# Moving the scaled copies of x and their trips behind the block's work on yi in a Mamba-2 scan, with the masked cb ahead of them

## The chip, the cores and the metric

The kernel runs on one core of one Trainium2 chip. The metric is the device time of one execution in microseconds (us). The engines are TensorE (PE, with its weight loads shown apart as PEld), VectorE (DVE), ScalarE (ACT), GpSimd (POOL) and SyncE (SP, which here only issues DMAs). Each engine works through its own list of instructions in order; when an instruction waits for a semaphore, everything behind it on that engine waits too.

## The reference

One layer of a hybrid network is computed for 256 frames of a new stream and 8 x 16 frames of running streams, 384 rows of 2048 in all, in float32:

```
u = RMSNorm(x);  P = u @ w_in            (columns: pool | z | x, B, C | dt | gates)
branch A: windowed means minus self, a linear map per group, a scale
branch B: x, B, C = silu(causal_conv(...));  y = ssd_scan(x, dt, A, B, C, h0) + D * x
          a = RMSNorm_per_group(y * silu(z))
m = sigmoid(gA) * (A @ w_pool_proj) + sigmoid(gB) * (a @ w_ssd_proj)
x += RMSNorm(m @ w_out);  x += RMSNorm(relu(RMSNorm(x) @ w_up)^2 @ w_down)
```

The change lies in the scan. Per group of heads it is, for a chunk with decays `cum`:

```
cb    = C @ B^T                                  (within the chunk)
y     = (cb * decay) @ (x * dt)  +  (C @ h) * exp(cum)
h_new = h * exp(last) + B^T @ (x * dt * w_end)
```

## The kernel before

The product with every weight is made of three matmuls: weight and activation are each split into a high and a low part, and high-high, high-low and low-high are added up (`mm3`). Weights come in half tiles of 128 x 1024 over SP's DMA queue (`wfetch`, line 63). ScalarE makes the high part (`wh`, line 70), VectorE the low part (`wl`, line 71); each of the three buffers in the chain has three slots. A projection of one 128-column tile uses two such halves of 24 matmuls (`half`, lines 98 to 100).

The phases are: the input norm and the pool branch (to about 410 us), the scan (to about 1220 us), the B gates, the output projections, and the MLP. The scan runs over 8 blocks, one for each of the 8 groups of heads; a block has 10 projections: two tiles of x, then B, C, two more tiles of x, and four of z. Its heads are handled as two pairs of x tiles, `D.p[0]` (called S) and `D.p[1]` (called S1). The code for S1 runs on into the next block as `prev.p[1]`.

Steps of the scan that matter here, by the names in the code:

- `conv` (a projection, `conv_in`, and `taps`): the result goes into `cbuf` (line 581), three taps are added in `cacc` (line 597) and a SiLU gives the tile `xs`.
- `xturned`: x is transposed within 32 x 32 blocks on VectorE (`xb`, line 612), spread to memory by four DMAs on POOL's queue (line 617) and fetched back as `xT` (line 623). The steps are placed one by one behind the halves of the next projections (`tick`).
- `xside`: from `xT` VectorE makes `xdt` and scales `xT` itself (line 738, four products of 128 x 384 for a pair), and `yis` from `yi` (line 745). The scaled `xT` is split into `xhl` (high part on ScalarE, line 752, low part on VectorE, line 753). Two DMAs on SP's queue take rows of it to memory (`x_scr`, line 756) and eight bring them back in another layout (`xst`, line 760).
- `mside`: VectorE multiplies `cb`, which lies in a PSUM bank, with the mask (`cbm`, line 731).
- `eside`: ScalarE builds the decays `E`, VectorE multiplies them with `cbm` (line 782). `dside` scales the state `hs` (line 785).
- On TensorE: `t_pp` (line 696, reads `xhl`), `t_cb` (line 652), `t_yT` (line 674, reads `yis`), `t_Y` (line 682, reads `xdt` and `E`), `t_yi` (line 661) and, in `state`, `t_su` (line 800, reads `xst` and `bst`), whose sums VectorE adds to `hs` (line 809). `final` gives `xs` (line 824) and the gated products (line 832).
- `bside` splits the transposed B (`Bhl`, lines 708 and 709) and sends it on its own trip through memory (lines 711 and 715).

In a block these TensorE steps stand in two bunches (`lump` keeps their order): after the projection of the third x tile come `t_pp` of the block before, `t_cb`, `t_yT` and `t_Y` of the block before, `t_yi` of S and `t_su` of the block before; after the last z projection come the same steps for S and `t_yi` for S1.

PSUM has two banks of tag `mm` (projections and `py`) and six of tag `ss` (`cb`, `Y`, `su` and others). `xT`, `xhl`, `xst`, `yis` and `cbm` have one buffer each, `xdt` two.

What sets the order: TensorE's order in the scan is that of the code (`last`, `chain`, `behind`). For the other engines a planner in the tile framework orders the instructions before the run. It goes by its own estimate of when an instruction is ready; of several that are ready, the one that stands earlier in the program goes first. A tile is handed on when its last reader is done.

Of the kernel before, what the change touches and what calls it, by code (L numbers as in the profile page):

```python
# [6 lines left out]
F32 = mybir.dt.float32  # L7
# [3 lines left out]
ALU = mybir.AluOpType  # L11
# [3 lines left out]
P = 128  # L15
# [18 lines left out]
def build(ctx, tc, io):  # L34
    nc = tc.nc
    v, s, te, gp, sy = nc.vector, nc.scalar, nc.tensor, nc.gpsimd, nc.sync
# [323 lines left out]
    tok = small.tile([P, 11, NH], F32, name="tok")  # L360
    decb = small.tile([P, NH, NB], F32, name="decb")
    with tc.tile_pool(name="phc", bufs=1, reuse_waits="tile") as pc, tc.tile_pool(name="phc2", bufs=2, reuse_waits="tile") as pc2:
        pst = pc.tile([P, KD, NB, 15], F32, name="pst")
        gp.dma_start(pst, io["state_pool"])
        bufs = []
# [192 lines left out]
    with tc.tile_pool(name="phd", bufs=2, reuse_waits="tile") as pd, tc.tile_pool(  # L558
        name="phd1", bufs=1, reuse_waits="tile"
# [32 lines left out]
        def taps(b, c, tag, nb):  # L592
            a = pd.tile([P, T], F32, tag="cacc", name=f"cacc{c}")
            w = lambda j: vec[:, V_CW + c * 4 + j : V_CW + c * 4 + j + 1]
            s.activation(seg(a), b[:, :, 0:16], AF.Copy, scale=w(0))
            for j in range(1, 4):
                v.scalar_tensor_tensor(
                    out=seg(a), in0=b[:, :, j : j + 16], scalar=w(j), in1=seg(a), op0=ALU.mult, op1=ALU.add
                )
            o = pd.tile([P, T], F32, tag=tag, name=f"xs{c}", bufs=nb)  # L600
            s.activation(o, a, AF.Silu, bias=vec[:, V_CB + c : V_CB + c + 1])
            return o

        def conv(ui, c, tag, nb):
            return taps(conv_in(ui, c), c, tag, nb)
# [19 lines left out]
        def xturned(D, g, j):  # L625
            S = D.p[j // 2]
            if j % 2 == 0:
                S.xT = pd.tile([P, 2, 3, P], F32, tag="xT", name=f"xT{S.nm}", bufs=1)
            turned(D.xs[j], g * 4 + j, S.xT[:, j % 2])
# [99 lines left out]
        def mside(D):  # L729
            D.cbm = pd.tile([P, 512], F32, tag="cbm", name=f"cbm{D.g}", bufs=1)  # L730
            v.tensor_tensor(D.cbm, D.cb, cst[:, C_MASK : C_MASK + 512], ALU.mult)

        def xside(S):
            S.xdt = pd.tile([P, 2, 3, P], F32, tag="xdt", name=f"xdt{S.nm}")
            for q in range(2):
                tv = S.xT[:, q].rearrange("p b (h q) -> p b h q", h=2)
                for o, i in ((S.xdt, 3), (S.xT, 6)):
                    v.tensor_tensor(
                        o[:, q].rearrange("p b (h q) -> p b h q", h=2),
                        tv,  # L740
                        tok[:, i : i + 3, S.h0 + q * 2 : S.h0 + q * 2 + 2].unsqueeze(3).to_broadcast([P, 3, 2, 64]),
                        ALU.mult,
                    )
            S.yis = pd.tile([P, 2, P], F32, tag="yis", name=f"yis{S.nm}", bufs=1)
            v.tensor_tensor(
                S.yis.rearrange("p j (h q) -> p (j h) q", h=2),
                S.yi.rearrange("p (h q) -> p h q", h=4),
                tok[:, 10, S.h0 : S.h0 + 4].unsqueeze(2).to_broadcast([P, 4, 64]),
                ALU.mult,
            )  # L750
            S.xhl = pd.tile([P, 2, 2, 3, P], F32R, tag="xhl", name=f"xhl{S.nm}", bufs=1)
            s.activation(S.xhl[:, 0], S.xT, AF.Copy)
            v.tensor_tensor(S.xhl[:, 1], S.xT, S.xhl[:, 0].bitcast(F32), ALU.subtract)
            xscr = x_scr[S.qd]
            for l in range(2):
                sy.dma_start(xscr[:, l], S.xhl[:, l, :, 2, :].bitcast(F32))
            S.xst = pd.tile([P, 4, 2 * P], F32R, tag="xst", name=f"xst{S.nm}", bufs=1)
            for p4 in range(4):
                for h2 in range(2):
                    sy.dma_start(  # L760
                        S.xst[h2 * 64 + p4 * 16 : h2 * 64 + p4 * 16 + 16].bitcast(F32),
                        xscr.rearrange("(q h r) l j n -> h l r q (j n)", q=4, h=2)[h2, p4 % 2],
                    )

        def eside(S, q):
            if q == 0:
                S.E = pd.tile([P, 4, 512], F32, tag="E", name=f"E{S.nm}", bufs=1)
            for hh in (q * 2, q * 2 + 1):
                ch = S.cbcs[q][:, hh % 2]
                s.activation(S.E[:, hh, P:TP], ch[:, P:TP], AF.Exp, bias=tok[:, 9, S.h0 + hh : S.h0 + hh + 1])  # L770
                for b, e0 in enumerate((0, TP, T)):
                    s.activation(
                        S.E[:, hh, e0 : e0 + P],
                        ch[:, b * P : b * P + P],
                        AF.Relu,
                        bias=tok[:, b, S.h0 + hh : S.h0 + hh + 1],
                        scale=-1.0,
                    )
            Eq = S.E[:, q * 2 : q * 2 + 2]
            s.activation(Eq[:, :, :P], Eq[:, :, :P], AF.Exp, scale=-1.0)  # L780
            s.activation(Eq[:, :, TP:], Eq[:, :, TP:], AF.Exp, scale=-1.0)
            v.tensor_tensor(Eq, Eq, S.D.cbm.unsqueeze(1).to_broadcast([P, 2, 512]), ALU.mult)
# [82 lines left out]
        prev = None  # L865
        for g in range(G + 1):
            if g == G:
                eside(prev.p[1], 0)
                eside(prev.p[1], 1)
                dside(prev.p[1])  # L870
                gate_b(0, pd, "hs")
                py = mmtile("pp_last")
                lump(lambda: t_pp(prev.p[1], py))
                lump(lambda: t_yT(prev.p[1]))
                lump(lambda: t_Y(prev.p[1]))
                state(prev.p[1])
                final(prev.p[1])
                gate_b(1, pd, "hs")
                finish(prev)
                break  # L880
            u0 = 17 + g * 10
            D = Pair()
            D.g = g
            D.p = [pair(D, jp) for jp in range(2)]
            D.xs, D.zs = [], []
            D.Bhl = pd.tile([P, 2, 3, P], F32R, tag="Bhl", name=f"Bhl{g}")
            D.xs.append(conv(u0, g * 4, "xs", 6))
            xturned(D, g, 0)
            pload(D.p[0])
            if g:  # L890
                eside(prev.p[1], 0)
            D.xs.append(conv(u0 + 1, g * 4 + 1, "xs", 6))
            xturned(D, g, 1)
            if g:
                eside(prev.p[1], 1)
            D.BT = conv(u0 + 2, 32 + g, "BT", 2)
            turned(D.BT, 32 + g, D.Bhl[:, 1].bitcast(F32))
            if g:
                dside(prev.p[1])
            cload(D.p[0])  # L900
            D.CT = conv(u0 + 3, 40 + g, "CT", 2)
            cside(D)
            b2 = conv_in(u0 + 4, g * 4 + 2)
            S = D.p[0]
            S.py = mmtile(f"py{S.nm}")
            if g:
                lump(lambda: t_pp(prev.p[1], S.py))
            lump(lambda: t_cb(D))
            bside(D)
            if g:  # L910
                lump(lambda: t_yT(prev.p[1]))
                lump(lambda: t_Y(prev.p[1]))
            lump(lambda: t_yi(S))
            xside(S)
            mside(D)
            if g:
                state(prev.p[1])
                final(prev.p[1])
            D.xs.append(taps(b2, g * 4 + 2, "xs", 6))
            xturned(D, g, 2)  # L920
            D.xs.append(conv(u0 + 5, g * 4 + 3, "xs", 6))
            xturned(D, g, 3)
            eside(S, 0)

            def zproj(j):
                ps = proj(in_units(u0 + 6 + j), xg, f"z{g}_{j}")
                z = pd.tile([P, T], F32, tag="zs", name=f"zs{g}_{j}", bufs=7)
                with later():
                    v.tensor_tensor(halves(z), even_odd(ps), halves(rstd), ALU.mult)  # L929
                    s.activation(z, z, AF.Silu)  # L930
                D.zs.append(z)

            zproj(0)
            pload(D.p[1])
            eside(S, 1)
            zproj(1)
            if g:
                finish(prev)
            zproj(2)
            dside(S)  # L940
            cload(D.p[1])
            zproj(3)
            S1 = D.p[1]
            S1.py = mmtile(f"py{S1.nm}")
            lump(lambda: t_pp(S, S1.py))
            lump(lambda: t_yT(S))
            lump(lambda: t_Y(S))
            lump(lambda: t_yi(S1))
            xside(S1)
            state(S)  # L950
            final(S)
            prev = D
# [92 lines left out]
    with tc.tile_pool(name="phf", bufs=1, side="right", reuse_waits="tile") as pf, tc.tile_pool(  # L1045
        name="phf2", bufs=2, side="right", reuse_waits="tile"
# [240 lines left out]
    with tc.tile_pool(name="phg", bufs=1, reuse_waits="tile") as pg, tc.tile_pool(  # L1287
# [9 lines left out]
        for c8 in range(NC):  # L1297
            hh = []
            for f8 in range(8):
                f = c8 * 8 + f8  # L1300
# [172 lines left out]
```

## Time and profile before

| | us |
|---|---|
| median of 3 runs | 2701.65 (2698.83 to 2708.1) |
| profiled execution, its own time | 2702.03 |
| span of the profile | 2700.1 |
| mean granted TensorE clock | 0.993 |

In the page, "busy" is the time in which an engine executed; a group's line is that of the kernel file. In a timeline row come the start in us from the begin of the span, the duration, the engine, the line, the operation, the tile written and those read, the shapes and a count; a bracket gives the idle time of the engine just before, and what ended it. In a row of the waits come the instruction that waited, what it waited for, the time in total, how often, and the longest. In a row of stretches come the busy times of the engines, each with its number of instructions, then the granted TensorE clock as a share of full speed, the busy share of the DMA engines and the GB/s. The whole page has TensorE at 98% and VectorE at 56% of the span; the scan, where the change lies, is one third of it.

### The profile page before, as it was taken

How to read it: one execution, taken by the hardware profiler on the slowest of the kernel's cores; microseconds unless marked ns; L12 is line 12 of the kernel's file. 1: busy time of each engine (PE TensorE's matmuls, PEld its weight loads, DVE VectorE, ACT ScalarE, POOL GpSimd, SP SyncE). 2: the span in 40 equal slices, each digit the busy share in tenths (PEclk: the TensorE clock that was granted, in tenths of full speed). 3: DMA queues.
4: the chain of work that ended last, by engine and by line, in shares of the span. 5: the costliest groups of instructions: out<-in, count | busy, mean ns of one | idle time of the engine just before them, and what ended most of it. 6: DMA issues, size and time to landing. Idle time of an engine off the chain costs nothing.

```text
span 2700.1 us, 38584 instructions
## 1 busy us (share of the span) xinstructions
PE 2647.5 (98%) x15149; PEld 2463.7 (91%) x15149; DVE 1524.7 (56%) x2148; ACT 1150.1 (43%) x1806; POOL 245.2 (9%) x366
## 2 busy tenths in 40 slices
PE   9999999899999899999999999999999999999998
PEld 9998889898999899988888888989999999999897
DVE  6585336687787787866433345634444444444446
ACT  6443235456565565644422234633233333333233
POOL 0000002223223223311000000000000000000000
PEclk9999999999999999999999999999999999999999
DMA  7444446666666676766644454333334444444443
GB/s 269 152 132 157 145 151 210 201 222 224 228 228 221 207 249 209 226 205 225 230 156 156 156 187 156 125 133 135 138 133 137 137 133 136 138 133 138 135 133 132
DMA packets 153845, 467.10 MB, mean 173 GB/s; under 512 B 21120, under 2 KB 48320, under 8 KB 148672
## 3 DMA queue, kind: packets, MB, share of 16 engines
q1 hardware_dynamic: 134400, 389.90, 44.1%
q0 software_dynamic: 19264, 74.74, 8.0%
q8 instruction: 119, 1.95, 0.3%
q14 instruction: 62, 0.51, 0.1%
HBM read 414.97 MB, written 49.58 MB: 172 GB/s over the span
## 4 chain that ended last, share of the span: by engine, by line
PE 55%; DVE 2%; DMA 1%; issue 1%; ACT 0%; POOL 0%; DVEq 0%; POOLq 0%; ACTq 0%
PE pj_up L98 6%; PE pj_up L100 6%; PE pj_up L99 6%; PE wd L151 6%; PE wd L150 6%; PE wd L149 6%; PE pj_sp L149 3%; PE pj_sp L150 3%; PE pj_sp L151 3%; PE wo L151 2%; PE wo L150 2%; PE pj_gb L149 2%; PE wo L149 2%; PE pj_gb L151 2%; PE pj_gb L150 2%
## 5 line engine op out<-in xcount | busy, mean ns | idle before, releaser
L98 PE MATMUL pj_up<-x1h,wh_up 128*128 128x384 f32 (+1 forms) x1024 | 333.7, 326 | 0.0
L99 PE MATMUL pj_up<-x1l,wh_up 128*128 128x384 f32 (+1 forms) x1024 | 333.4, 326 | 0.0
L100 PE MATMUL pj_up<-x1h,wl_up 128*128 128x384 f32 (+1 forms) x1024 | 333.4, 326 | 0.0
L71 DVE TENSOR_TENSOR wl_wd<-w_wd,wh_wd 128x1024 fp32r<-128x1024 f32 x126 | 154.3, 1225 | 240.5 <-ACT wh_wd L70 240.5
L149 PE MATMUL wd<-wh_wd,hh 128*128 128x512 f32 x756 | 286.5, 379 | 0.0
L150 PE MATMUL wd<-wl_wd,hh 128*128 128x512 f32 x756 | 286.5, 379 | 0.0
L151 PE MATMUL wd<-wh_wd,hl 128*128 128x512 f32 x756 | 286.5, 379 | 0.0
L70 ACT ACTIVATE wh_wd<-w_wd 128x1024 fp32r<-128x1024 f32 x126 | 133.1, 1057 | 322.3 <-PE wd L151 261.9
L98 PE MATMUL pj_x<-xgh,wh_x 128*128 128x384 f32 x768 | 256.1, 333 | 2.6 <-DVE zs L929 2.6
L70 ACT ACTIVATE wh_up<-w_up 128x1024 fp32r<-128x1024 f32 x126 | 133.1, 1057 | 291.8 <-PE pj_up L99 231.8
L100 PE MATMUL pj_x<-xgh,wl_x 128*128 128x384 f32 x768 | 254.3, 331 | 1.0 <-DVE wl_x L71 1.0
L71 DVE TENSOR_TENSOR wl_up<-w_up,wh_up 128x1024 fp32r<-128x1024 f32 x126 | 154.3, 1225 | 177.9 <-ACT wh_up L70 177.7
L99 PE MATMUL pj_x<-xgl,wh_x 128*128 128x384 f32 x768 | 254.2, 331 | 0.0
L99 PEld LDWEIGHTS pj_up<-x1l,wh_up 128*128 128x128 f32 x1024 | 193.6, 189 | 0.2
L98 PEld LDWEIGHTS pj_up<-x1h,wh_up 128*128 128x128 f32 x1024 | 193.6, 189 | 0.2
L100 PEld LDWEIGHTS pj_up<-x1h,wl_up 128*128 128x128 f32 x1024 | 193.6, 189 | 0.0
L100 PE MATMUL pj_z<-xgh,wl_z 128*128 128x384 f32 x512 | 168.4, 329 | 12.6 <-DVE wl_z L71 12.5
L98 PE MATMUL pj_z<-xgh,wh_z 128*128 128x384 f32 x512 | 167.6, 327 | 0.8 <-ACT wh_z L70 0.8
L99 PE MATMUL pj_z<-xgl,wh_z 128*128 128x384 f32 x512 | 167.5, 327 | 0.0
L71 DVE TENSOR_TENSOR wl_sp<-w_sp,wh_sp 128x1024 fp32r<-128x1024 f32 x64 | 78.4, 1225 | 154.0 <-ACT wh_sp L70 154.0
L151 PEld LDWEIGHTS wd<-wh_wd,hl 128*128 128x128 f32 x756 | 142.9, 189 | 20.3
L149 PEld LDWEIGHTS wd<-wh_wd,hh 128*128 128x128 f32 x756 | 142.9, 189 | 20.1
(333 smaller groups left out, 5979.7 us busy)
## 6 DMA issues: line engine op xcount, KB each, us to landing
w_up<-w_up SPq DMA_DIRECT2D x128, 512.0 KB, 3.3
w_wd<-w_down SPq DMA_DIRECT2D x128, 512.0 KB, 3.3
w_x<-w_in SPq DMA_DIRECT2D x96, 512.0 KB, 4.5
w_z<-w_in SPq DMA_DIRECT2D x64, 512.0 KB, 3.9
w_sp<-w_ssd SPq DMA_DIRECT2D x64, 512.0 KB, 3.3
w_ga<-w_ga SPq DMA_DIRECT2D x32, 512.0 KB, 3.3
w_pp<-w_pp SPq DMA_DIRECT2D x32, 512.0 KB, 3.3
hs<-ssm POOLq DMA_DIRECT2D x16, 1024.0 KB, 7.1
```

The source lines that it names most:

```text
L70: cut[0] = s.activation(h, w, AF.Copy)
L71: cut[1] = v.tensor_tensor(l, w, h.bitcast(F32), ALU.subtract)
L98: te.matmul(out, wh, xh, start=first, stop=False, **how)
L99: te.matmul(out, wh, xl, start=False, stop=False, **how)
L100: return te.matmul(out, wl, xh, start=False, stop=last, **how)
L149: te.matmul(out, mh, vh, start=k == 0, stop=False)
L150: te.matmul(out, mh, vl, start=False, stop=False)
L151: last[0] = te.matmul(out, ml, vh, start=False, stop=k == nk - 1)
```

## The change

`yis` leaves `xside` and becomes a step of its own, `yside`, at the old place of `xside`. In the first half of a block `mside` now stands ahead of it. What is left of `xside` (the scaled copies, their split and the trip to memory and back) comes later: for S behind the state update and the closing step of the block before and behind the taps of the third x tile, ahead of the projection of the fourth; for S1 behind the first projection of the next block, or, after the last block, at the head of the closing part.

```diff
+        def yside(S):
+            S.yis = pd.tile([P, 2, P], F32, tag="yis", name=f"yis{S.nm}", bufs=1)
+            v.tensor_tensor(
+                S.yis.rearrange("p j (h q) -> p (j h) q", h=2),
+                S.yi.rearrange("p (h q) -> p h q", h=4),
+                tok[:, 10, S.h0 : S.h0 + 4].unsqueeze(2).to_broadcast([P, 4, 64]),
+                ALU.mult,
+            )
+
         def xside(S):
...
-            S.yis = pd.tile([P, 2, P], F32, tag="yis", name=f"yis{S.nm}", bufs=1)
-            v.tensor_tensor(
...
-            )
...
         for g in range(G + 1):
             if g == G:
+                xside(prev.p[1])
                 eside(prev.p[1], 0)
...
             D.xs.append(conv(u0, g * 4, "xs", 6))
+            if g:
+                xside(prev.p[1])
             xturned(D, g, 0)
...
             lump(lambda: t_yi(S))
-            xside(S)
             mside(D)
+            yside(S)
             if g:
                 state(prev.p[1])
                 final(prev.p[1])
             D.xs.append(taps(b2, g * 4 + 2, "xs", 6))
+            xside(S)
             xturned(D, g, 2)
...
             lump(lambda: t_yi(S1))
-            xside(S1)
+            yside(S1)
             state(S)
             final(S)
```

More of the change, by code (lines that the diff above doesn't have):

```diff
@@ L743, in xside @@
                     )
-            S.yis = pd.tile([P, 2, P], F32, tag="yis", name=f"yis{S.nm}", bufs=1)
[L745 to L749, printed above, removed]
-            )
             S.xhl = pd.tile([P, 2, 2, 3, P], F32R, tag="xhl", name=f"xhl{S.nm}", bufs=1)
```

## The prediction

> **What bounds the kernel now.** I read the page first (busy shares), then the chain of waits, then the timelines of one block of the scan, then the clock in the stretches where TensorE had waited. Blocks are numbered 0 to 7, S is the first and S1 the second half of a block.
>
> ```profile
> span 2700.1 us, 38584 instructions
> PE 2647.5 (98%) x15149; PEld 2463.7 (91%) x15149; DVE 1524.7 (56%) x2148; ACT 1150.1 (43%) x1806; POOL 245.2 (9%) x366
> ```
>
> TensorE is the bound: 98% busy. Its order is fixed by the code and is not touched, so only its idle time and its slow time can move. What it waited for, and VectorE's longest wait in the scan (total, times, longest):
>
> ```profile
> DVE xdt L738 <- DMA xT<-t_scr: 69.1, 18, 6.2
> PE su L800 <- DVE cbm L731: 17.8, 6, 5.8
> PE pj_z L100 <- DVE wl_z L71: 12.5, 6, 7.1
> ```
>
> The largest TensorE wait is the state update `su` behind VectorE's `cbm`, in six of the eight blocks: `su` wants a PSUM bank that `cb` holds until `cbm` has read it. The second is the low part of a z weight. Block 3, TensorE and then VectorE:
>
> ```profile
> 746.29 0.60 PE L800 MATMUL su<-xst,bst 64*128 64x256 f32 x5
> 750.20 0.79 PE L800 MATMUL su<-xst,bst 64*128 64x256 f32 x3 [3.31 <-DVE cbm L731]
> 751.72 0.53 PE L100 MATMUL pj_x<-xgh,wl_x 128*128 128x384 f32 x1
> 777.66 0.33 PE L100 MATMUL pj_z<-xgh,wl_z 128*128 128x384 f32 x1
> ```
>
> ```profile
> 746.45 0.56 DVE L709 TENSOR_TENSOR Bhl<-Bhl 128x384 fp32r<-128x384 f32 x1 [2.37 <-ACT Bhl L708]
> 746.93 0.62 DVE L581 TENSOR_TENSOR cbuf<-pj_x,rstd 128x192 f32<-128x192 f32 x2
> 747.46 1.21 DVE L71 TENSOR_TENSOR wl_z<-w_z,wh_z 128x1024 fp32r<-128x1024 f32 x1
> 748.59 0.95 DVE L753 TENSOR_TENSOR xhl<-xT,xhl 128x768 fp32r<-128x768 f32 x1
> 749.46 0.68 DVE L731 TENSOR_TENSOR cbm<-cb,cst 128x512 f32<-128x512 f32 x1
> 750.06 1.13 DVE L824 SCALAR_TENSOR_TENSOR xs<-xs,vec,Y 128x384 f32<-128x384 f32 x2
> ...
> 751.58 0.42 DVE L745 TENSOR_TENSOR yis<-py,tok 128x256 f32<-128x256 f32 x1
> ...
> 755.30 2.28 DVE L785 TENSOR_TENSOR hs<-hs,decb 128x2048 f32<-128x2048 f32 x1
> ...
> 774.21 0.56 DVE L738 TENSOR_TENSOR xdt<-xT,tok 128x384 f32<-128x384 f32 x1 [3.45 <-DMA xT<-t_scr]
> ```
>
> Two things are to be seen. Ahead of `cbm` stand `Bhl`, which had come 2.37 us late, `cbuf`, one weight and the low part of `xhl`; the last alone belongs to the step that the change moves. Blocks 1 to 7 have this order alike. And the order is not that of the program: `yis` stands ahead of `cbm` there and runs 2.1 us behind it, `xdt` of S1 stands behind the fourth z projection and runs in the second. The planner starts what it takes for ready, and the place in the program only decides between two that are ready.
>
> The granted clock after the stalls (columns: stretch, its length, busy us and count of PE, PEld, DVE, ACT, POOL, then the clock):
>
> ```profile
> 653.80:660.70 6.90, 4.51 (x15) 4.29 (x16) 6.90 (x12) 5.72 (x16) 1.57 (x3) 0.51 0.59 174
> 749.30:756.30 7.00, 6.10 (x20) 5.88 (x21) 7.00 (x13) 5.65 (x15) 2.53 (x4) 0.51 0.64 189
> 844.90:848.40 3.50, 3.50 (x13) 3.50 (x12) 3.50 (x8) 3.07 (x11) 1.68 (x3) 0.51 0.40 120
> 943.90:947.40 3.50, 3.50 (x14) 3.42 (x12) 3.50 (x8) 2.34 (x9) 1.54 (x2) 0.51 0.50 145
> 1036.70:1040.20 3.50, 3.41 (x21) 3.29 (x22) 3.50 (x8) 2.33 (x8) 1.25 (x2) 1.00 0.52 159
> 1131.60:1135.10 3.50, 3.50 (x12) 3.28 (x13) 3.50 (x8) 2.35 (x8) 1.45 (x2) 0.51 0.52 180
> ```
>
> Half clock follows the stall in blocks 2, 3, 4, 5 and 7, not in 6. Half clock loses half of the busy time, so 4.5 / 2 + 6.1 / 2 + 3 x 3.5 / 2 = 10.5 us.
>
> **The change part by part.** *The four products of `xside` (L738).* 0.56 us each, 64 in all. They lose rank, but already run when the planner believes x has landed, long ahead of their place in the program, and what outranks them only now (the su additions, `final`, the taps) is not ready then. I cost the move at nothing, and the 69.1 us of waits on the xT trip stay. If the cover goes, one block's product pair costs 1.1 us of VectorE.
>
> *`cbm` ahead of `xhl`.* With `xside` behind the taps, `cbm` outranks the low part of `xhl`; on ScalarE the copies into `cbuf` also outrank its high part, so it is ready later still. `cbm` starts at 748.59 instead of 749.46, 0.87 us sooner; `Bhl`, `cbuf` and `wl_z` outrank it in both programs and stay ahead. Six stalls by 0.87 is 5.2 us off the 17.8. From below: nothing, if the planner keeps `xhl` first. From above: all 17.8.
>
> *What is late next.* Later in the same block TensorE comes to the first half of the third z projection, whose low part stands in VectorE's order behind `xdt` of S1. Its matmuls and that low part, block by block:
>
> ```profile
> 586.26 0.43 PE L100 MATMUL pj_z<-xgh,wl_z 128*128 128x384 f32 x1 [1.56 <-DVE wl_z L71]
> 682.88 0.33 PE L100 MATMUL pj_z<-xgh,wl_z 128*128 128x384 f32 x1
> 870.68 0.43 PE L100 MATMUL pj_z<-xgh,wl_z 128*128 128x384 f32 x1 [0.49 <-DVE wl_z L71]
> 970.81 0.43 PE L100 MATMUL pj_z<-xgh,wl_z 128*128 128x384 f32 x1 [0.87 <-DVE wl_z L71]
> 1063.58 0.43 PE L100 MATMUL pj_z<-xgh,wl_z 128*128 128x384 f32 x1 [2.06 <-DVE wl_z L71]
> ```
>
> ```profile
> 680.62 1.22 DVE L71 TENSOR_TENSOR wl_z<-w_z,wh_z 128x1024 fp32r<-128x1024 f32 x1
> 775.28 1.22 DVE L71 TENSOR_TENSOR wl_z<-w_z,wh_z 128x1024 fp32r<-128x1024 f32 x1
> 1160.08 0.56 DVE L738 TENSOR_TENSOR xdt<-xT,tok 128x384 f32<-128x384 f32 x1 [6.20 <-DMA xT<-t_scr]
> ```
>
> Blocks 1, 4, 5 and 6 wait here already, most of all 1 and 6, which lost least before it: what TensorE wins at `su` it waits for here. Blocks 2 and 3 have 682.88 - 681.84 = 1.04 and 777.66 - 776.50 = 1.16 us to spare. From `Bhl` to that low part VectorE does the same work in both kernels; `xhl` only changes sides with `cbm`. So blocks 2 and 3 keep their spare time, 2.2 us in all (0.87 from `cbm`, the rest from a shorter slow stretch); blocks 4 to 7 keep nothing if VectorE sets that point, 0.87 each if ScalarE does (its squares wait for VectorE's products of z, which may come sooner): I take half, 4 x 0.43 = 1.7.
>
> *The trips.* Per half block two writes to `x_scr` and eight reads into `xst` on SP's queue, moved with `xside`; the reads wait besides until `su` has read the one `xst` buffer:
>
> ```profile
> 753.44 5.45 SPq L760 DMA_DIRECT2D xst<-x_scr x8
> 760.03 8.86 SPq L63 DMA_DIRECT2D w_z<-w_in x3
> ```
>
> ```profile
> 757.55 1.06 ACT L70 ACTIVATE wh_z<-w_z 128x1024 fp32r<-128x1024 f32 x1 [1.43 <-PE pj_x L99]
> 771.23 1.04 ACT L70 ACTIVATE wh_z<-w_z 128x1024 fp32r<-128x1024 f32 x1
> ```
>
> Behind them is the weight fetch of 760.03, which ScalarE takes up at 771.23. A trip that ends 2 us later delays that fetch by about 1 us of those 11. S's rows are wanted by `su` at the end of the block, S1's four projections after the new place. Cost: nothing; with that cover gone, the delay itself, 1 to 3 us a block. SP waits for no one else here; POOL's queue gets nothing new.
>
> *`yis` and the products after it.* 0.42 us, still behind `t_yi`: nothing.
>
> *The end of the scan.* The first B gate waits for `xs`, which runs behind `xhl`:
>
> ```profile
> 1180.07 1.13 DVE L824 SCALAR_TENSOR_TENSOR xs<-xs,vec,Y 128x384 f32<-128x384 f32 x2
> 1180.82 0.45 PE L149 MATMUL pj_gb<-wh_gb,xgh 128*128 128x512 f32 x1 [3.05 <-DVE xs L824]
> ```
>
> Between 0 and 0.87 us sooner; I take 0.5.
>
> *Sum.* 2.2 + 1.7 + 0.5 = 4.4 us. The profiled run took 2702.03 us (its span and 1.9 us around it), 0.4 above the median of 2701.65: 2697.6 against the first, and I give 2697.
>
> *The clock, by rule and by row.* The stretches above show half clock after stalls of 5.8 and 3.3 us and after three short ones, while 1.9 us in block 6 had none:
>
> ```profile
> PE su L800 <- DVE cbm L731: 2.0, 1, 2.0
> PE su L800 <- DVE cbm L731: 1.9, 1, 1.9
> ```
>
> The Trainium skill ("TensorE: Matmul & The Clock Gate", section "HAM oscillation") says in my words that TensorE falls to half clock only after an idle gap of more than about 3.4 us. By that rule blocks 4, 5 and 7 would have no slow stretch to win; the trace disagrees (0.51 after 2.0 us in block 7), so the measurement decides. The first rival below would then be worth 6.1 us and lie within the measurement.
>
> **Rivals.** *The gain is kept.* If the x trip of S1 moves forward with TensorE, the six times 0.87 us stay, the three short slow stretches vanish with stalls near 1.2 us (3 x 1.75 = 5.3) and the end gives 0.9: 11.4 us, 2691. For it: block 6, stall 1.9, no slow stretch. Against: the four waits at the third z projection. *All of it goes.* The planner finds `cbm` ready before `Bhl`: 17.8 + 10.5 = 28.3 us, 2674. Against: `Bhl` and `cbuf` outrank it. *Slower: the x trip of S1 slips.* `xhl` now falls among the taps of the third x tile or behind them; if it and the 2.28 us of L785 come ahead of the fourth tile's transposition, the planned place of `xdt` is too early for the data, as in block 7, where it waits 6.20 us instead of 3.45. 2.75 us more in blocks 1, 4, 5 and 6, less 1.1 spare in 2 and 3: 4 x 2.75 + 2 x 1.65 = 14.3 us, 2716. It decides once the slip is over 1.4 us a block (8.1 / 6). For it: four blocks have no spare time. Against: the same VectorE work in sum. *The order stays as it is:* 2702.
>
> **How the numbers follow.** Given back as costed 0.40, kept 0.28, all gone 0.08, slower 0.21, unchanged 0.03. 0.3% (8.1 us) is about what a measurement of this kernel can tell from no change: faster 0.28 + 0.08 = 0.36, same 0.43, slower 0.21. The likeliest case's own range is 2693 to 2702 (0.87 kept in every block, or nothing). For 8 in 10 the low end is 2682, beyond the kept gain with one or two stalls gone whole; the high end 2715, nearly the whole of the slip; the case of all gone and a worse slip are left out.
>
> **What would show it.** Right: VectorE's `cbm` directly behind `wl_z` and ahead of `xhl`; the `su` waits at about 12 to 13 us; the z waits of blocks 1 and 4 to 6 up by up to 0.87 each; `xdt` waits near 69 us. Wrong: `cbm` behind `xhl` still (unchanged), `su` waits near 0 (all gone), z waits above 20 us or new waits on `wl_x` or `wl_z` (slip), or VectorE's `xdt` in another stretch of the block, which would upset the part that I cost at nothing.

## The result, and the profile after

| | before | changed |
|---|---|---|
| first comparison, median us | 2705.72 (2698.83 to 2708.84) | 2696.58 (2692.62 to 2701.01) |
| ratio, 95% interval | | 0.9969 (0.9957 to 0.998) |
| second comparison, median us | 2696.59 (2689.72 to 2702.86) | 2691.6 (2687.39 to 2696.8) |
| ratio, 95% interval | | 0.9984 (0.9973 to 0.9994) |
| profiled execution, its own time | 2702.03 | 2697.46 |
| its span | 2700.1 | 2695.3 |
| its mean granted clock | 0.993 | 0.992 |

The change makes the kernel faster by 0.2 to 0.3%. The kernel before has other medians in the two comparisons (2705.72 and 2696.59), so only ratios within one are used below.

The busy times on the page of the changed kernel:

```profile
PE 2650.0 (98%) x15149; PEld 2468.2 (92%) x15149; DVE 1523.1 (57%) x2148; ACT 1186.8 (44%) x1834; POOL 269.6 (10%) x366
```

Its waits, in the same form as those shown of before (total, times, longest):

```profile
DVE xdt L747 <- DMA xT<-t_scr: 53.9, 18, 4.8
PE pj_z L100 <- DVE wl_z L71: 16.1, 7, 5.1
PE su L802 <- DVE cbm L731: 14.9, 6, 4.7
```

The wait at `su` fell by 2.9 us, that at z rose by 3.6: what the first gained, the second took. These three waits of the trace of before are gone (with 0.8 us on `wh_z` and 0.3 on `hs`), and that of `cb` on `xs` is 1.2 us shorter (2.7):

```profile
PE pj_gb L149 <- DVE xs L824: 3.0, 1, 3.0
PE pj_x L98 <- DVE zs L929: 2.6, 1, 2.6
PE pj_x L100 <- DVE wl_x L71: 1.0, 1, 1.0
```

VectorE in block 3 of the changed kernel, to be laid beside the rows of 746 to 775 us of before:

```profile
747.17 0.56 DVE L709 TENSOR_TENSOR Bhl<-Bhl 128x384 fp32r<-128x384 f32 x1 [4.44 <-ACT Bhl L708]
...
748.18 1.22 DVE L71 TENSOR_TENSOR wl_z<-w_z,wh_z 128x1024 fp32r<-128x1024 f32 x1
749.31 0.69 DVE L731 TENSOR_TENSOR cbm<-cb,cst 128x512 f32<-128x512 f32 x1
...
756.20 0.96 DVE L755 TENSOR_TENSOR xhl<-xT,xhl 128x768 fp32r<-128x768 f32 x1
...
775.91 0.56 DVE L747 TENSOR_TENSOR xdt<-xT,tok 128x384 f32<-128x384 f32 x1 [4.07 <-DMA xT<-t_scr]
776.50 0.56 DVE L747 TENSOR_TENSOR xT<-xT,tok 128x384 f32<-128x384 f32 x1
776.98 2.35 DVE L71 TENSOR_TENSOR wl_z<-w_z,wh_z 128x1024 fp32r<-128x1024 f32 x2
```

`cbm` stands directly behind `wl_z`, and `xhl` 7 us behind it, as forecast. But the row that leads the fence has moved too: `Bhl` comes 4.44 us late, where it was 2.37 us late before. In this block `su` therefore waits longer than before (4.30 against 3.31), although one instruction less stands ahead of `cbm`. At the other end of the fence the low part of the z weight runs without a pause behind the two products of x, and these had waited 4.07 us for `xT`; the rows of blocks 4 to 7 are the same, with waits for `xT` of 2.54 to 4.79 us. TensorE's two stalls in block 3, and those at the third z projection in blocks 5, 6 and 7:

```profile
750.05 0.80 PE L802 MATMUL su<-xst,bst 64*128 64x256 f32 x3 [4.30 <-DVE cbm L731]
778.25 0.43 PE L100 MATMUL pj_z<-xgh,wl_z 128*128 128x384 f32 x1 [0.84 <-DVE wl_z L71]
963.95 0.69 PE L100 MATMUL pj_z<-xgh,wl_z 128*128 128x384 f32 x1 [2.67 <-DVE wl_z L71]
1058.09 0.43 PE L100 MATMUL pj_z<-xgh,wl_z 128*128 128x384 f32 x1 [3.17 <-DVE wl_z L71]
1155.13 0.69 PE L100 MATMUL pj_z<-xgh,wl_z 128*128 128x384 f32 x1 [2.51 <-DVE wl_z L71]
```

Blocks 5 and 6 had 0.87 and 2.06 us there, block 3 had 1.16 us to spare. Block 7 had no such stall: its 2.51 us stand against the 3.05 us at the first B gate, which are gone. The total of z hides a part of the rise: block 0, where no wait at `su` comes before it, fell from 7.12 to 5.09 us, and blocks 1 to 7 together rose by 5.7.

**A ledger.** Two things can be added up from each trace between 440 and 1300 us (the scan): TensorE's waits, and the time in which the clock record grants half speed, whose cost is put at 0.49 of its length (the rows of stretches show 0.50 and 0.51). Before had 41.9 us of waits and 30.7 us at half clock, after has 33.7 and 37.5. The difference is -8.2 + 0.49 x 6.8 = -4.9 us; the span fell by 4.8. So in this profile the waits that went were worth 8.2 us, and the clock took 3.3 of it back: the stalls at z in blocks 5, 6 and 7 each have a slow stretch. In a second profile of the changed kernel the waits fell by 8.5 us and the half clock fell too, by 3.4 us, so the part of the waits repeats and that of the clock does not. The same sum for every kernel measured (the rows below "changed" are the experiments):

| kernel | waits, us | half clock, us | span, us | span - waits - 0.49 x half clock |
|---|---|---|---|---|
| before | 41.9 | 30.7 | 2700.1 | 2643.2 |
| changed | 33.7 | 37.5 | 2695.3 | 2643.2 |
| changed, second comparison | 33.4 | 27.3 | 2691.4 | 2644.6 |
| mask only | 38.0 | 27.3 | 2696.8 | 2645.4 |
| first pair only | 32.0 | 37.5 | 2691.0 | 2640.6 |
| second pair only | 37.8 | 27.3 | 2695.2 | 2644.0 |
| copies pinned | 29.3 | 41.0 | 2689.1 | 2639.7 |
| mask ahead of Bhl | 35.8 | 34.1 | 2694.8 | 2642.3 |
| Bhl later | 32.6 | 27.3 | 2689.8 | 2643.8 |
| both off the path | 5.8 | 3.4 | 2649.8 | 2642.3 |
| both off, again | 4.2 | 3.4 | 2647.1 | 2641.2 |
| before, both off | 4.6 | 3.4 | 2646.7 | 2640.4 |

The last column stays within 2639.7 to 2645.4 while the span moves by 53 us: waits and half clock are the whole difference between these kernels, to about 3 us. It is no finer than that, and the match of 4.9 with 4.8 us is closer than it deserves: a slow stretch often begins inside a stall, and that part is counted in both columns (TensorE was busy in 24.0 of the 30.7 us before and in 34.4 of the 37.5 after).

The table's waits also show the exchange better than one pair of profiles can. In the kernel before, both profiles of the changed one, and the kernels with the mask only, one pair only and the mask ahead of `Bhl`, the wait at `su` is anything from 8.9 to 17.8 us and that at z from 12.5 to 23.5, but the two together are always 28.4 to 32.4.

### The profile page after: what moved, and what is told of

Its sections match the earlier page's. It is cut to its first block, busy times and chain, and to the rows that moved or that the text cites. A ratio compares the mean times of both kernels' runs of the same rounds, so it can differ in the third digit from the quotient of the medians.

```text
span 2695.3 us, 38595 instructions
## 1 busy us (share of the span) xinstructions
PE 2650.0 (98%) x15149; PEld 2468.2 (92%) x15149; DVE 1523.1 (57%) x2148; ACT 1186.8 (44%) x1834; POOL 269.6 (10%) x366
## 4 chain that ended last, share of the span: by engine, by line
PE 56%; DMA 1%; DVE 1%; POOL 0%; issue 0%; ACT 0%; DVEq 0%; POOLq 0%; ACTq 0%
PE pj_up L98 6%; PE pj_up L100 6%; PE pj_up L99 6%; PE wd L150 6%; PE wd L151 6%; PE wd L149 6%; PE pj_sp L151 3%; PE pj_sp L150 3%; PE pj_sp L149 3%; PE pj_gb L149 2%; PE wo L149 2%; PE wo L151 2%; PE pj_gb L150 2%; PE pj_gb L151 2%; PE wo L150 2%; DMA t_scr<-xb 1%
## 5 line engine op out<-in xcount | busy, mean ns | idle before, releaser
L150 PEld LDWEIGHTS wd<-wl_wd,hh 128*128 128x128 f32 x756 | 143.2, 189 | 19.8
```

The lines of the kernel that those rows point to most:

```text
L150: te.matmul(out, mh, vl, start=False, stop=False)
```

## The experiments

The theory under test, from the prediction: what TensorE wins at `su` it waits for again at the third z projection, because VectorE stands there in its order behind a transfer (`xdt` of S1 waits for `xT`). The rival: the gain at `su` is kept. The kernels with the mask only, with one pair only and with the copies pinned ran side by side with the kernel before at 2696.91 us; the changed kernel once more, the two with `Bhl` moved and the first with both off the path at 2696.59; the last two at 2700.74.

The changed kernel once more:

> The changed kernel once more, beside the experiments of this call, so that ratios can be taken within the call. Every theory: 0.995 to 0.999 of the kernel before, since the first comparison gave 0.9969 and the kernel before alone moved by 9 us between the two calls.

Measured: 2691.6 us, 0.9984, as in the table at the head. Its waits are 18.7 us at z and 11.0 at `su`: two profiles of one kernel differ by 2.6 and 3.9 us in these, so a reading below is firm only where the difference is larger or several kernels agree.

**Mask only.** The kernel before, with one swap:

```diff
-            xside(S)
             mside(D)
+            xside(S)
```

> The kernel before with the masked cb ahead of the whole old x step, nothing else: in VectorE's order only cbm and the low part of xhl change places in each block. Give-back theory: TensorE's wait of su for cbm falls from 17.8 to about 13 us, its wait for the low part of the z weights rises from 12.5 to about 15.5 us, the time falls by 1 to 3 us. If the gain is kept: the z wait stays at 12.5 us and the time falls by 5 to 11 us.

Measured: 2696.85 us, ratio 0.9994 (0.9984 to 1.0005). The waits of TensorE:

```profile
PE pj_z L100 <- DVE wl_z L71: 15.8, 7, 4.9
PE su L800 <- DVE cbm L731: 13.4, 5, 5.3
```

The swap alone takes 4.4 us from `su`, near the 5.2 that six blocks at 0.87 us give, and z takes 3.3 of them back. The rest is too small to be told from nothing. The first term of the prediction and the give-back both appear with no other part of the change, though each is hardly more than two profiles of one kernel differ by.

**First pair only.** The changed kernel, with S1's copies back at their old place:

```diff
             if g == G:
-                xside(prev.p[1])
                 eside(prev.p[1], 0)
...
-            if g:
-                xside(prev.p[1])
             xturned(D, g, 0)
...
             yside(S1)
+            xside(S1)
```

> The changed kernel, but the second pair's scaled copies stay at their old place at the end of the block. Give-back theory: nearly the whole change, su wait near 15 us and z wait near 16 us, time 2 to 5 us below before. If the gain comes from the second pair (its output product ahead of the split at the block's end and at the first B gate), this is within 2 us of before, and the gate's wait of 3.0 us behind the output product stays.

**Second pair only.** The changed kernel, with S in the old order (`yis`, copies, mask):

```diff
-            mside(D)
             yside(S)
+            xside(S)
+            mside(D)
...
             D.xs.append(taps(b2, g * 4 + 2, "xs", 6))
-            xside(S)
```

> The kernel before, with only the second pair's scaled copies moved behind the first projection of the next block; the first pair and cbm stay. Give-back theory: su wait stays at 17.8 and z wait at 12.5 us, time 0 to 1 us below before. If the gain comes from the second pair: the gate's wait of 3.0 and the wait of 2.6 us for a z product are gone, time 4 to 6 us below before.

Measured: first pair 2693.37 us, 0.9989 (0.998 to 0.9998); second pair 2696.98 us, 1.0005 (0.9996 to 1.0014). So what the change gains comes with the first pair; moving S1's copies is worth nothing that can be measured. The waits tell the same: 10.3 us at `su` and 18.5 at z with the first pair alone, 15.6 and 12.8 (nearly those of before) with the second alone. The 2.6 us of `pj_x` behind `zs` and the wait of the first B gate behind `xs` are still there with the second pair alone (1.9 and 2.5 us) and with the mask alone (2.7 and 1.1); they are missing with the first pair alone and in both profiles of the changed kernel. They go with the deferral of S's copies.

**Copies pinned.** The changed kernel, with each call of `xside` made to follow, on its engines, the weight halves issued last before it (`later` is the helper by which the code already does this for projections):

```diff
-                xside(prev.p[1])
+                with later():
+                    xside(prev.p[1])
```

(and the same for the other two calls).

> The changed kernel, with the scaled copies held in VectorE's and ScalarE's order behind the weight split that stands last ahead of their place in the program, so that they can't run early and wait there for xT. If VectorE's wait for xT sets the third z projection and makes Bhl late: the wait of xdt for xT falls from 53.9 to under 10 us, the z wait from 16.1 to under 5 us, the su wait from 14.9 to under 8 us, time 12 to 30 us below before. If VectorE's amount of work sets these points: the xT wait goes, but z and su waits stay near 16 and 15 us, and the time stays within 5 us of the changed kernel.

Measured: 2689.67 us, 0.997 (0.9961 to 0.9979). The wait on `wl_z` is gone, and the wait of `xdt` for `xT` with it. So it was VectorE's wait, in order, for the tile's trip that held the third z projection. But the other half of the expectation failed: `su` was to fall under 8 us and rose to 25.8, and of the 12 to 30 us 7.2 came. The time is not better than the changed kernel's by more than the measurement tells. ScalarE and VectorE show whose wait it is that grew:

```profile
PE su L802 <- DVE cbm L731: 25.8, 7, 5.6
ACT Bhl L708 <- DMA Bhl<-t_scr: 43.9, 8, 6.6
DVE Bhl L709 <- ACT Bhl L708: 32.4, 8, 5.4
```

Before, the second of these rows stood at 19.0 us and the third at 13.9. `Bhl` is made from B's transposed tile, which makes the same kind of trip through memory as x, and `cbm` stands behind the copy of it. VectorE in block 3 shows what the pinned products add:

```profile
744.57 0.56 DVE L709 TENSOR_TENSOR Bhl<-Bhl 128x384 fp32r<-128x384 f32 x1 [5.00 <-ACT Bhl L708]
745.04 0.55 DVE L747 TENSOR_TENSOR xT<-xT,tok 128x384 f32<-128x384 f32 x1
...
748.11 0.68 DVE L731 TENSOR_TENSOR cbm<-cb,cst 128x512 f32<-128x512 f32 x1
```

Three of S's four products (745.04, 745.51 and 746.51) now run between the late `Bhl` and `cbm`. From ScalarE's copy of `Bhl` to `cbm` pass 4.10 us in each of blocks 1 to 7, against 2.69 or 2.70 in the changed kernel, which makes 9.9 us over the seven blocks; the wait at `su` grew by 10.9. The copy itself is no later in blocks 2 to 7 (20.4 us in sum behind the first matmul of `cb`, 21.7 in the changed kernel), only in block 1 (3.5 us behind it, where it had been 0.5 ahead). The prediction had seen `Bhl` ahead of `cbm` in block 3 and had taken it as given.

**Mask ahead of Bhl.** Which engine's order holds `cbm`? In the changed kernel VectorE's part of `Bhl` is put behind `cbm`:

```diff
             lump(lambda: t_cb(D))
-            bside(D)
+            with behind(mside(D)):
+                bside(D)
...
             lump(lambda: t_yi(S))
-            mside(D)
             yside(S)
```

(`mside` returns its instruction.)

> The changed kernel, with cbm put ahead of the low part of Bhl on VectorE, directly behind the matmuls that make cb; on ScalarE the copy into Bhl still stands ahead of the weight half that cbm follows. Theory A (su is held by the transfer that fills Bhl, through whichever queue its copy stands in): VectorE's place alone does little, since ScalarE's copy still holds the weight half ahead of cbm; su's wait on cbm stays within 2 us of the changed kernel's 14.9 and the time within 2 us of it. Theory B (su is held by VectorE's subtraction for Bhl): su's wait falls by the 4 to 5 us of blocks 3 and before to under 6 in all, and the time by up to 5 us or, if it is given back at z, by 1 to 2.

Measured: 2691.56 us, against 2691.6 of the changed kernel beside it; 0.9985 and 0.9984. The `su` wait is 8.9 us, against 11.0 in the changed kernel's profile of this comparison, and z has 23.5 against 18.7. The time is as the first theory said; the size of the `su` wait is not, it came out 6.0 us below the 14.9, but the changed kernel alone differs by 3.9 between its own two profiles. What holds `cbm` in this kernel shows in block 3, first VectorE, then ScalarE:

```profile
747.60 1.22 DVE L71 TENSOR_TENSOR wl_z<-w_z,wh_z 128x1024 fp32r<-128x1024 f32 x1 [3.08 <-ACT wh_z L70]
748.74 0.68 DVE L731 TENSOR_TENSOR cbm<-cb,cst 128x512 f32<-128x512 f32 x1
```

```profile
746.10 0.53 ACT L708 ACTIVATE Bhl<-Bhl 128x384 fp32r<-128x384 f32 x1 [3.37 <-DMA Bhl<-t_scr]
746.52 1.04 ACT L70 ACTIVATE wh_z<-w_z 128x1024 fp32r<-128x1024 f32 x1
```

`cbm` stands ahead of `Bhl` on VectorE now (whose part follows at 749.34) and is still late: it stands behind `wl_z`, that waits for `wh_z`, and that stands on ScalarE behind its own copy of `Bhl`. The wait changed engines: over all blocks VectorE's wait for ScalarE's copy of `Bhl` fell from 14.9 to 1.3 us, and that of `wl_z` for `wh_z` rose from 8.4 to 22.8.

**Bhl later.** So `Bhl` was taken out of both orders, in the changed kernel:

```diff
             lump(lambda: t_cb(D))
-            bside(D)
...
             D.xs.append(conv(u0 + 5, g * 4 + 3, "xs", 6))
+            with later():
+                bside(D)
             xturned(D, g, 3)
```

> The changed kernel, with the copy into Bhl, its subtraction and its eight transfers put behind the weight halves of the fourth x projection, so that neither ScalarE nor VectorE waits for Bhl ahead of cbm. The products of x keep their places. Theory A (su is held by Bhl's transfer, and what is won there is given back at the third z projection, where wl_z stands behind xdt): su's wait on cbm falls from 14.9 to under 4, z's on wl_z rises from 16.1 to 24 or more, and the time falls by 0 to 4 us below the changed kernel. Rival (won at su and kept): z stays at 14 to 18 and the time falls by 10 us or more. Rival (something other than Bhl holds cbm): su stays above 10.

Measured: 2693.94 us, 0.9993 (0.9983 to 1.0003). The wait at `su` is gone from the list altogether, and nothing is gained (the expected 0 to 4 us below the changed kernel came out as 2.3 above it, with intervals that overlap):

```profile
PE pj_z L100 <- DVE wl_z L71: 23.6, 7, 5.2
PE bc_g L197 <- DVE nl_g L193: 5.8, 5, 3.7
```

The waits of TensorE sum to 32.6 us, against 33.4 in the changed kernel. This is the give-back at its plainest: all 11.0 us at `su` were won, and the same time later in the block z and the norm's broadcast took 10.7 (4.9 and 5.8). VectorE in block 3 shows why: `xdt` waits longer for the same tile, and `wl_z` comes behind it.

```profile
772.78 0.56 DVE L747 TENSOR_TENSOR xdt<-xT,tok 128x384 f32<-128x384 f32 x1 [6.59 <-DMA xT<-t_scr]
...
775.65 1.22 DVE L71 TENSOR_TENSOR wl_z<-w_z,wh_z 128x1024 fp32r<-128x1024 f32 x1
```

**Both off the path.** The last edit and the pinned copies together:

> The same edit of Bhl, in the kernel with the copies of x pinned behind the weight halves, so that no weight half or mask stands behind a transposed tile's transfer. Theory A (the block's two losses are VectorE's and ScalarE's waits in order for transfers, which hand the same microseconds to one another): su's wait falls from 25.8 to under 5, z's stays under 3, and the time falls 15 to 26 us below the kernel with pinned copies alone, to 0.988 to 0.992 of the kernel before. Rival (a third wait takes it: the transfers of weights, or the second scan matmuls for the late products): under 6 us below the kernel with pinned copies, with a wait of TensorE that now stands near zero grown to over 10 us.

Measured: 2650.29 us, 0.9833 (0.9816 to 0.985), more than the 15 to 26 us that were expected below the pinned copies. All waits of TensorE in the scan:

```profile
PE pj_x L98 <- DVE cbuf L581: 2.5, 1, 2.5
PE cb L652 <- ACT xs L601: 1.3, 1, 1.3
PE bc_g L197 <- DVE nl_g L193: 1.3, 2, 0.8
PE pj_x L100 <- DVE wl_x L71: 0.7, 1, 0.7
```

The expectation had counted the waits (25.8 less some) and a part of the clock. The ledger gives it in full: 23.5 us of waits and 0.49 x 37.6 = 18.4 us of half clock less than with the copies pinned alone make 41.9; the spans differ by 39.3. (With half of TensorE's busy time in the slow stretches, 34.3 and 3.4 us, as their cost, the sum is 39.) Against the kernel before, the changed kernel with `Bhl` later stood at 0.9993 and with the copies pinned at 0.997; with both it stands at 0.9833. Each of the two edits alone was tried in the changed kernel only.

**Both off, again, and in the kernel before.** Is the change needed for it? The same two edits in the kernel before, whose order of copies, `yis` and mask is kept:

```diff
             lump(lambda: t_cb(D))
-            bside(D)
...
             lump(lambda: t_yi(S))
-            xside(S)
+            with later():
+                xside(S)
             mside(D)
...
             D.xs.append(conv(u0 + 5, g * 4 + 3, "xs", 6))
+            with later():
+                bside(D)
...
-            xside(S1)
+            with later():
+                xside(S1)
```

> The kernel before, its order of x copies, yis and cbm kept, with the two edits of the last experiment alone: the products and parts of x pinned behind the weight halves that were last issued, and the copy into Bhl behind the fourth x projection. Theory A (the change's own reordering only handed stalls between su and z; what counts is that no weight half or mask stands behind a transfer's wait): TensorE's waits in the scan fall from 42 to under 12, the stretches at half clock from 27-31 us to under 10, the time to 0.983 to 0.988 of the kernel before, within 8 us of the kernel that has the change as well. Rival (the deferral by one projection is needed for it): z's or su's wait stays above 10 and the time above 0.992 of the kernel before.

> The changed kernel with both waits off once more, for a closer interval in the same call: 0.982 to 0.985 of the kernel before. By the sum found so far (span = about 2643 us, and TensorE's waits in the scan, and half of the stretches there at half clock) its span is 2643 + 6 + 2 = 2651; if the gain had another cause than those two, the waits and the stretches would not add up to it again.

Measured side by side: 2648.31 us for the kernel before with the edits, 0.9805 (0.9791 to 0.9818), and 2648.53 us for the changed one, 0.981 (0.9796 to 0.9824). They are the same, and both are faster than the kernel before and the changed one; both are a little below what was expected (0.983 to 0.988 and 0.982 to 0.985). The changed one's span of 2647.1 us, with 4.2 us of waits and 3.4 at half clock, leaves 2641.2 in the ledger: it adds up again, to 2 us of the 2643 that was set. The wait at `su` and VectorE in block 3 of the kernel before with the edits:

```profile
PE su L800 <- DVE cbm L731: 0.4, 1, 0.4
```

```profile
726.91 1.22 DVE L71 TENSOR_TENSOR wl_z<-w_z,wh_z 128x1024 fp32r<-128x1024 f32 x1
728.04 0.95 DVE L753 TENSOR_TENSOR xhl<-xT,xhl 128x768 fp32r<-128x768 f32 x1
728.91 0.68 DVE L731 TENSOR_TENSOR cbm<-cb,cst 128x512 f32<-128x512 f32 x1
```

`xhl` stands ahead of `cbm` here, with its 0.95 us, just as in the kernel before, and `su` waits 0.4 us in the whole scan. The place of `xhl`, on which the change and the prediction turned, costs nothing once neither of the two transfers is waited for in order.

## Why the prediction was right

Forecast were 2697.0 us and no change beyond 0.3% as the likeliest; the profiled run took 2697.46, and the ratios of 0.9969 and 0.9984 lie just past that bound and within it. The likeliest case, given back in part, is what happened. But the terms of its sum are not the terms that the trace shows, and that the total was met within 0.5 us is luck: 2.2 + 1.7 us came out as -0.7, 0.5 as 5.7, and small waits of 3.3 us and 3.3 us of clock, none of them in the sum, cancel.

- **`cbm` 0.87 us sooner: right in place.** It stands where it was said to stand. The mark was 12 to 13 us of waits at `su`; the two profiles of the changed kernel, 14.9 and 11.0, lie on either side of it, the swap alone gave 13.4. Block by block the stalls do not show the 0.87 (from 1.3 us less in blocks 5 and 6 to 1.0 more in block 3), since the lateness of `Bhl`, which I held constant, moves by more than that. But counted from ScalarE's copy of `Bhl`, `cbm` starts after 3.56 or 3.57 us in each of blocks 1 to 7 before and after 2.69 or 2.70 in the changed kernel and with the mask alone: the term itself is exact.
- **The give-back: right in kind, too small in size.** I let blocks 2 and 3 keep 2.2 us and blocks 4 to 7 half of theirs, and said that the z waits of blocks 1 and 4 to 6 would rise by up to 0.87 each. At the third z projection those of blocks 1 and 4 fell a little (by 0.10 and 0.08), those of blocks 5 and 6 rose by 1.80 and 1.11, and blocks 3 and 7 got stalls of 0.84 and 2.51 us that they had not had. In sum `su` won 2.9 and z lost 3.6 (6.8 and 6.2 in the second profile): the two terms that I put at 2.2 + 1.7 us came to -0.7 (0.6). The step that failed is the half that I allowed for ScalarE: in blocks 3 to 7 `wl_z` ran directly behind the products of x on VectorE, and what these waited for was the transfer of `xT`. Nor did that transfer follow TensorE: counted from the matmul that ends the stall at `su`, the products began after 23.4 to 24.9 us in blocks 2 to 6 before and after 24.3 to 25.9 in the changed kernel (28.6 and 26.6 in block 7).
- **The end of the scan: undersized.** I gave 0.5 us, since `xhl` only steps aside for `xs`. The whole 3.05 us at the first B gate went, with the 2.62 of `pj_x` behind `zs`, which I had not costed at all. The runs of one pair tie both to the deferral of S's copies. The second goes back to a transfer once more. In block 4 of the kernel before, VectorE waits for the second tile of S1's `xT`; the group norm stands behind that, its products in `zs` (line 845, at 887.22) leave for memory late, and the fourth z product waits for the buffer:

```profile
878.71 0.56 DVE L738 TENSOR_TENSOR xdt<-xT,tok 128x384 f32<-128x384 f32 x1 [4.62 <-DMA xT<-t_scr]
893.10 0.56 DVE L929 TENSOR_TENSOR zs<-pj_z,rstd 128x384 f32<-128x384 f32 x1 [2.55 <-DMA a_scr<-zs]
893.81 0.40 PE L98 MATMUL pj_x<-xgh,wh_x 128*128 128x384 f32 x1 [2.62 <-DVE zs L929]
```

The wait of 4.62 us is there with the mask alone (4.42) and the second pair alone (4.19), and so is the stall; both are gone with the first pair alone and in the changed kernel, where the fourth z product waits 0.75 us for its buffer. Why the tile comes back sooner there was not traced. The two stalls make up what the give-back lost: without them the sum would have been near zero.
- **The clock.** I priced half clock only where it might vanish, in a rival. It grew by 6.8 us and cost 3.3 in the profiled run, and shrank by 3.4 us in the second profile: what the change does to it is open.
- **The products of x at nothing, waits on `xT` near 69 us: both were off.** The waits came out at 53.9 and 49.8 us. With the mask alone they are 65.1, with the second pair 65.4, with the first pair 51.8: this too goes with S. Of the 15 us, block 4 lost 7.0 (waits of 4.94 and 4.62 us became one of 2.54), blocks 5, 6 and 7 lost 2.0, 1.0 and 1.4, and blocks 0 and 1 1.2 and 1.0. One of these waits is the one that was worth 2.62 us at `pj_x`, so moving the products was not without effect.
- **The trips at nothing: right.** S's reads come later and the weights behind them too, and no TensorE wait on a weight's transfer appears. SP's queue in block 3, to be laid beside 753.44 and 760.03 of before:

```profile
757.62 7.32 SPq L762 DMA_DIRECT2D xst<-x_scr  x7
764.99 2.87 SPq L63 DMA_DIRECT2D w_z<-w_in  x3
```

- **The rivals.** "The gain is kept" would have wanted the x trip of S1 to move forward with TensorE; by the 24.3 to 25.9 us above it did not, except in block 7. "All of it goes" I gave 0.08 and refused since `Bhl` outranks `cbm`; when the wait of `Bhl` was removed, the `su` wait did go whole, and the 28.3 us that I gave for it did not come, since z and the norm's broadcast took them. The slip of the x trip did not come either: `xhl` did fall among the taps (756.20, right behind the third), ahead of L785 as I had said for it, and z waits stayed at 16 to 19 us instead of above 20.

What I missed is the reading that the last experiments give. I saw two stalls and asked what each instruction in VectorE's order costs (0.56, 0.87, 1.21 us), while both stalls began with a bracket of several us that leads to a transfer: `Bhl` 2.37 us (through ScalarE's copy of it) and `xdt` 3.45 us in the rows that I quoted. TensorE's pace in a block was set by the trips of B's and x's tiles, which had to be back before weights split behind them could be used, and shifting 0.87 us of work ahead of either trip could only move a stall from one to the other.

## What to carry to other kernels

Where an engine that works in order prepares operands for TensorE and also waits for transfers, look first at the brackets on transfers: taking a wait of one transfer away wins next to nothing as long as the next one in the loop still holds the same engines (0.9993 and 0.997 for each alone), and wins much when the last of them is out of the way (0.981 for both). Put the consumer of a late transfer behind the work that TensorE wants next, and let it wait there. And price a stall with what follows it: here the waits of 42 us and the half clock behind them, 31 us at 0.49, added up to 57 us, most of which could be had.

## What the runs showed of the hardware

**Half clock after short stalls.** In the changed kernel all stalls in the scan of 1.83 us and more had a stretch at half clock that began within 2 us of their end, some of them before it; those of 1.46 us and less (six, in blocks 1 and 3 to 7) had none of their own. Behind the stall of 1.83 us that ends at 1126.20 (columns: stretch, its length, busy us and count of PE, PEld, DVE, ACT, POOL, then the granted clock):

```profile
1127.60:1130.90 3.30, 3.30 (x12) 3.30 (x11) 3.30 (x8) 2.33 (x8) 1.54 (x2) 0.50 0.58 200
```

It is no fixed threshold. With the mask only, a stall of 1.44 us (to 844.18) was followed by a slow stretch 1.30 us later, and one of 3.19 us (to 970.04) by none. The kernel before had stalls of 2.62 us (to 893.81) and 3.05 us (to 1180.82) without one, and none followed its stall of 2.06 us at 1063.58 either:

```profile
1063.60:1067.00 3.40, 3.40 (x21) 3.40 (x22) 3.40 (x6) 0.52 (x1) 0.04 (x1) 1.00 0.77 234
```

In all twelve profiles every stall of 3.28 us and more in the scan had a slow stretch. The stretches are 3.41 us long or twice that (6.83), and once three times (10.24, with the first pair only). What decides between 1.4 and 3.2 us was not tried.

**More table loads on ScalarE, at no cost.** Not foreseen: with S's copies deferred, the SiLU of the third x tile falls between the exponentials of `E`, and ScalarE changes its function table more often. Of before, and then of the changed kernel:

```profile
L770 ACT ACT_TABLE_LOAD x17 | 21.8, 1283 | 0.3
L601 ACT ACT_TABLE_LOAD x17 | 21.8, 1283 | 0.3
```

```profile
L772 ACT ACT_TABLE_LOAD x24 | 30.8, 1283 | 0.4
L601 ACT ACT_TABLE_LOAD x24 | 30.8, 1283 | 0.4
L783 ACT ACT_TABLE_LOAD x7 | 9.0, 1283 | 0.1
L936 ACT ACT_TABLE_LOAD x7 | 9.0, 1283 | 0.1
```

28 loads at 1.283 us are 35.9 us more of ScalarE's time (1150.1 to 1186.8 us busy). None of it shows in TensorE's waits: the changed kernel with both waits off has them, the kernel before with both off has 14 fewer and keeps ScalarE busy for 21.4 us less, and the two take the same time. One switch in block 3 of the changed kernel:

```profile
756.10 0.51 ACT L839 ACTIVATE ysq<-zs 128x384 f32<-128x384 f32 x1
756.62 1.28 ACT L601 ACT_TABLE_LOAD   x1
757.92 0.61 ACT L601 ACTIVATE xs<-cacc,vec 128x384 f32<-128x384 f32 x1
```

The Trainium skill ("ScalarE: Activation LUTs", section "What ACT_TABLE_LOAD costs") gives 1283 ns for the load and about 1380 ns more for a drain with every switch. The trace agrees with the first to the digit; of the second these rows show nothing: from the end of one activation (756.61) to the start of the next (757.92) pass 1.31 us.
